# RWKV-7 in a hybrid block: two chunks of the recurrence to a tile, values dumped apart, GpSimd's decay by chunk

## The chip, the cores and the metric

The kernel runs on one core of a Trainium2 chip. Its engines work side by side, each through its own queue in a fixed order: TensorE (PE, with its weight loads as PEld), VectorE (DVE), ScalarE (ACT), GpSimd (POOL) and SyncE (SP), which here does little but start DMAs. The metric is the time of one execution on the device in microseconds, the median of several runs. The profile comes from one further execution.

## The reference

One layer of a block with three mixers (HGRN2, RWKV-7 and MLA attention) and a gated feed-forward part; 512 tokens, width 1024, fp32. The change is in the RWKV-7 mixer, which has 16 heads of size 64:

```python
h = rms_norm(x, mix_pre_g[l])
z = h @ w_cols
o_hg = hgrn2_mixer(...)
o_rw, v_first = rwkv7_mixer(...)
o_mla = mla_mixer(...)
merged = (g_hg * (o_hg @ w_branch[l, 0]) + g_rw * (o_rw @ w_branch[l, 1]) + g_mla * (o_mla @ w_branch[l, 2]))
x = x + rms_norm(merged @ w_out[l], mix_post_g[l])
...
# rwkv7_mixer, for each token t:
sa = einsum('bhvk,bhk->bhv', state, -kk_t)
state = state * w_t + sa[..., None] * (kk_t * a_t) + v_t[..., None] * k_t
y_t = einsum('bhvk,bhk->bhv', state, r_t)
...
y = (group_norm(y) * lnx_g + lnx_b + bonus) * g
```

## The kernel before

Every large product is made of three matmuls, because each fp32 operand is split into a high and a low part (`mm3`, L137 to L141). A weight slab of 256 KB comes by DMA into `wsD`; ScalarE casts the high part `whD` (L207), VectorE subtracts the low part `wlD` (L134). The input projections run as a stream of such groups, with result `mmD`, from the start until about 955 us.

The other work is woven into this stream. The order on each engine is fixed when the kernel is built: instructions carry a priority (a "lane") and a scheduler lays them out; buffers that come free late move what needs them. Two things tie the engines together beyond the data:

- `pace` (L143 to L155) makes GpSimd write a small `token` (L151) after each three dense matmuls, and lets a group start only when the token of the fifth group before it is written (`PACE = 5`). So whatever holds GpSimd holds back the tokens behind it.
- A tile is taken from a pool with a number of buffers. Who writes into a buffer again waits for the last reader of what was in it, a DMA too.

RWKV-7 is computed in chunks of 64 tokens (NC = 8 chunks, C = 64), and the 16 heads go in 8 pairs, two pairs to a group. For each group `rwkv_group` takes a tile `G` (two buffers) that holds for two pairs and all chunks five fields of 128 columns: X (two), LM, PV and BKT. PV has two halves; GpSimd sets the one that will hold the state's part to zero (L449). `rwkv_prep` fills the fields for one pair:

- tile `lw` (one buffer) gets its first column from GpSimd (L527) and the rest from ScalarE (L528);
- GpSimd multiplies BK by the decay of the next chunk (L599), TensorE transposes it, and ScalarE copies it into BKT (L604);
- the gate goes to DRAM (`grw`, L623);
- the values are transposed and copied into PV by ScalarE (L632).

`rwkv_inverse` inverts triangular blocks through DRAM (`Ld`, `Td`, tile `inv`), `rwkv_merge` assembles them in tile `TR`. Then the group's fields are dumped chunk by chunk to `rwd`: 28 DMAs of 640 KB and 4 of 512.

When all groups are done, `rwkv_chain` goes through the 8 chunks in order. `load(c)` fetches one chunk into a tile `CH` (three buffers). In each chunk TensorE makes `z` from X and PV (L714), VectorE copies it to `zsb` (L716), TensorE applies the inverse (L724), and the result goes back into PV: one half by VectorE (L725), the other by ScalarE (L726). From it comes the next chunk's state, which is written into that chunk's PV (L734, L736), and the output `y` (L738, L740). A last loop adds the bonus and multiplies by the gate, both fetched into `CH` tiles.

The attention's rotary angles (L922 to L931) are small VectorE steps that run in this neighbourhood: three steps on `angk`, five or six on `angr`, then a sine on ScalarE; once for sine, once for cosine, on the same two tiles. The program takes RWKV-7's pools (`rwkv_open`) before HGRN2's (`hgrn_open`).

Of the kernel before, what the change touches and what calls it, by code (L numbers as in the profile page):

```python
# [17 lines left out]
ALU = mybir.AluOpType  # L18
# [4 lines left out]
P = 128  # L23
S = 512
# [11 lines left out]
C = 64  # L36
NC = S // C
# [1 line left out]
DECAY = math.exp(-0.5)  # L39
HG_LEVELS = (1, 2, 4, 8, 16)  # L40
HB = 32

RWC = 5 * P
PACE = 5
SCALE = 192.0 ** -0.5

# [58 lines left out]
class Kern:  # L105
# [299 lines left out]
    def rwkv_open(self, e1, e2, e3):  # L405
        tc = self.tc
        pool = lambda es, name, bufs, **kw: es.enter_context(tc.tile_pool(name=name, bufs=bufs, **kw))
        self.gp = pool(e2, "rwG", 1, side="right")
        self.pC, self.pY = (pool(e1, n, 1, space=PSUM, side="right") for n in ("pC", "pY"))
        self.rt = pool(e3, "rt", 1)  # L410
        self.pR = pool(e3, "pR", 2, space=PSUM)


        self.gC = self.t(self.cpool, [P, 8, NC], "gC")
        self.rwd = [self.t(self.dpool, [NC, P, 2, RWC], f"rwd{g}") for g in range(4)]

    def shifted(self, dst, j):

# [22 lines left out]

    def rwkv_group(self, g):

        all_ = self.t(self.gp, [P, 2, NC, RWC], "G", bufs=2)
        G = self.fields(all_)
        G["all"] = all_
        for e in range(2):

            self.nc.gpsimd.memset(G["PV"][e][e * 64:e * 64 + 64], 0.0)  # L449
        G["Ld"] = self.t(self.dpool, [64, 32, 32], "Ld", bufs=2)  # L450
        G["Td"] = self.t(self.dpool, [64, 32, 32], "Td", bufs=2)
        for q in range(2):
            self.lane(5)
            self.rwkv_prep(G, 2 * g + q, q)
        self.lane(3)
        self.rwkv_inverse(G, g)
        self.rwkv_merge(G, g)
        for c in range(NC):
            n = RWC if c < NC - 1 else RWC - P
            self.dumps.append((self.rwd[g][c][:, :, :n], all_[:, :, c, :n]))  # L460
        if g == 3:
            while self.dumps:
                self.nc.sync.dma_start(*self.dumps.pop(0))
# [10 lines left out]

    def fields(self, t):

        return {"X": [t[..., e * P:(e + 1) * P] for e in range(2)], "LM": t[..., 2 * P:3 * P],
                "PV": [t[..., 3 * P + e * C:3 * P + (e + 1) * C] for e in range(2)], "BKT": t[..., 4 * P:]}

    def rwkv(self, e1, e2, e3):  # L480
        self.lane(5)
        self.rwkv_lora()
        self.dumps = []
        for g in range(4):
            self.rwkv_group(g)
        e2.close()
        self.rw = e1.enter_context(self.tc.tile_pool(name="rwC", bufs=1, side="right"))
        self.lane(1)
        self.rwkv_chain()
# [11 lines left out]
    def rwkv_prep(self, G, p, q):  # L501
        nc, rt = self.nc, self.rt
        V, A, Pl = nc.vector, nc.scalar, nc.gpsimd
        ins = self.ins
        H = [slice(0, 64), slice(64, 128)]
        f = slice(p * P, (p + 1) * P)
# [19 lines left out]
        lw = self.t(rt, [P, NC, C + 1], "lw")  # L526
# [11 lines left out]
        gC = self.gC[:, p]  # L538
# [28 lines left out]
        BK = self.t(rt, [P, NC, P], "BK")  # L567
        X = G["X"]
# [13 lines left out]
        LM = G["LM"]  # L582
# [9 lines left out]
        for e in range(2):  # L592
            for b in range(2):
                rows = slice(e * 64 + b * 32, e * 64 + b * 32 + 32)
                o = ((q * 2 + e) * 2 + b) * NC
                nc.sync.dma_start(G["Ld"][o:o + NC].rearrange("c s t -> s c t"), LM[rows, q, :, b * 32:b * 32 + 32])

        n = NC - 1
        Pl.tensor_tensor(BK[:, :n], BK[:, :n], gC[:, 1:].unsqueeze(2).to_broadcast([P, n, P]), op=ALU.mult)  # L599
        for cc in range(0, n, 4):  # L600
            m = min(4, n - cc)
            pt = self.t(self.pR, [P, 4, P], "pr")
# [18 lines left out]
        g = self.t(rt, [P, S], "v")  # L621
# [3 lines left out]
        pv = self.t(self.pR, [P, S], "pr")  # L625
        for i in range(NT):
            nc.tensor.transpose(pv[:, i * P:(i + 1) * P], v[:, i * P:(i + 1) * P], self.ident)
        pv4 = pv.rearrange("t (i h d) -> t i h d", i=NT, h=2)
        for e in range(2):
            dst = G["PV"][e][H[1 - e], q].rearrange("t (i j) d -> t i j d", j=2)  # L630
            for j in range(2):
                A.copy(dst[:, :, j, :], pv4[H[j], :, e, :])  # L632

    def rwkv_inverse(self, G, g):

# [23 lines left out]
    def rwkv_merge(self, G, g):  # L659

        nc, LM = self.nc, G["LM"]
        V, A = nc.vector, nc.scalar
        TR = self.t(self.gp, [P, 2, NC, 32], "TR")
        pR = self.t(self.pY, [P, 2, NC, 32], "yb")
        pM = self.t(self.pY, [P, 2, NC, 32], "yb")
        R = [[slice(e * 64 + o, e * 64 + o + 32) for o in (0, 32)] for e in range(2)]
        qc = [(q, c) for q in range(2) for c in range(NC)]
        for r0, _ in R:
            V.transpose(TR[r0], LM[r0, :, :, 0:32])
        self.side_by_side(  # L670
            partial(nc.tensor.matmul, pR[r1, q, c, :], lhsT=LM[r0, q, c, 32:64], rhs=TR[r0, q, c, :], start=True, stop=True,
                    tile_position=(r0.start, r1.start))
            for q, c in qc for r0, r1 in R)
        for _, r1 in R:
            A.copy(TR[r1], pR[r1])
        self.side_by_side(
            partial(nc.tensor.matmul, pM[r0, q, c, :], lhsT=TR[r1, q, c, :], rhs=LM[r1, q, c, 32:64], start=True, stop=True,
                    tile_position=(r1.start, r0.start))
            for q, c in qc for r0, r1 in R)
        for r0, _ in R:  # L680
            A.copy(LM[r0, :, :, 32:64], pM[r0])

    def rwkv_chain(self):

        nc, rw = self.nc, self.rw
        V, A, Pl = nc.vector, nc.scalar, nc.gpsimd
        mm = nc.tensor.matmul
        H = [slice(0, 64), slice(64, 128)]
        heads = [(p, e) for p in range(8) for e in range(2)]
        chunks = []  # L690

        def load(c):
            t = self.t(rw, [P, 8, RWC], "CH", bufs=3)
            n = RWC if c < NC - 1 else RWC - P
            for g in range(4):
                nc.sync.dma_start(t[:, 2 * g:2 * g + 2, :n], self.rwd[g][c][:, :, :n])
            chunks.append(self.fields(t))

        load(0)
        St = self.t(rw, [P, 8, C], "St")  # L700
# [1 line left out]
        for c in range(NC):  # L702
            if c < NC - 1:
                load(c + 1)
            G = chunks[c]
# [38 lines left out]
                self.lane(1)  # L744
        self.lane(3)

        bv, gr, out = (self.t(rw, [P, 8, RWC], "CH", bufs=3) for _ in range(3))
        for p in range(8):
            nc.sync.dma_start(bv[:, p, :S], self.bv[p])
            nc.sync.dma_start(gr[:, p, :S], self.grw[p])  # L750
        for p in range(8):
            pt = self.t(self.pC if p % 2 else self.pY, [P, S], "zus" if p % 2 else "yb")
            for i in range(NT):
                nc.tensor.transpose(pt[:, i * P:(i + 1) * P], y[:, i, p].rearrange("t e d -> t (e d)"), self.ident)
            o = out[:, p, :S]
            o4 = o.rearrange("f (i j t) -> f i j t", j=2, t=C)
            pt4 = pt.rearrange("f (i j t) -> f i j t", j=2, t=C)
            lb, lg = self.vec("rwkv_lnx_b", p), self.vec("rwkv_lnx_g", p)
            A.activation(o[H[0]], pt[H[0]], AF.Identity, bias=lb[H[0]], scale=lg[H[0]])
            for j in range(2):  # L760

                A.activation(o4[H[1], :, j, :], pt4[H[1], :, 1 - j, :], AF.Identity, bias=lb[H[1]], scale=lg[H[1]])
            V.tensor_tensor(o, o, bv[:, p, :S], op=ALU.add)
            V.tensor_tensor(o, o, gr[:, p, :S], op=ALU.mult)
            nc.sync.dma_start(self.orw[p], o)
            self.dump(f"orw{p}", o)

# [515 lines left out]
    def run(self):  # L1283
        self.full = True
        self.lane(7)
        self.setup()
        es = self.ctx
        self.stream_open(es)
        pes, bes = ExitStack(), ExitStack()
        self.stream_psum(pes, 2)  # L1290
        self.norm_in()
        self.dense_z(RW_OFF + 3072, halves=True)
        for n in range(0, 1024, 256):
            for o in (1024, 0, 2048):
                self.dense_z(RW_OFF + o + n)
            for o in (HG_OFF[1], HG_OFF[0], HG_OFF[2], HG_OFF[3]):
                self.dense_z(o + n)
        for o, n in ((0, 256), (256, 256), (512, 192)):
            self.dense_z(CQ_OFF + o, n)
        for n in (*range(8, 16, 2), *range(0, 8, 2), *range(16, 24, 2)):  # L1300
            self.dense_gate(n)
        e1, e2, e3, e4, e5, oes = (ExitStack() for _ in range(6))
        self.rwkv_open(e1, e2, e3)
        self.hgrn_open(e4)
        self.rwkv(e1, e2, e3)
        for h in range(8):
# [51 lines left out]
```

## Time and profile before

| | |
|---|---|
| median of 3 runs | 1423.61 us (1423.25 to 1424.04) |
| profiled execution, its own time | 1427.17 us |
| its span, first to last instruction | 1425.4 us |
| mean granted clock of TensorE | 0.986 of full speed |
| busy: PE, DVE, ACT, POOL | 96%, 60%, 45%, 12% of the span |
| DMA | 235.80 MB, 165 GB/s |

Times in the trace count from the span's start. A row of the timeline reads: start, duration, engine, line, operation, result <- operands, shape, count; in brackets stands the idle time of the engine before it and what ended it. `q` behind an engine's name is its sequencer, which waits, branches and starts DMAs. The granted clock is given in tenths of full speed on the page and as a fraction of it for a stretch of time.

### The profile page before, as it was taken

How to read it: one execution, taken by the hardware profiler on the slowest of the kernel's cores; microseconds unless marked ns; L12 is line 12 of the kernel's file. 1: busy time of each engine (PE TensorE's matmuls, PEld its weight loads, DVE VectorE, ACT ScalarE, POOL GpSimd, SP SyncE). 2: the span in 40 equal slices, each digit the busy share in tenths (PEclk: the TensorE clock that was granted, in tenths of full speed). 3: DMA queues.
4: the chain of work that ended last, by engine and by line, in shares of the span. 5: the costliest groups of instructions: out<-in, count | busy, mean ns of one | idle time of the engine just before them, and what ended most of it. 6: DMA issues, size and time to landing. Idle time of an engine off the chain costs nothing.

```text
span 1425.4 us, 27298 instructions
## 1 busy us (share of the span) xinstructions
PE 1365.3 (96%) x9664; PEld 1110.6 (78%) x9664; DVE 853.2 (60%) x1756; ACT 638.5 (45%) x1259; POOL 165.6 (12%) x1000
## 2 busy tenths in 40 slices
PE   6999989898999999999999999999999999999998
PEld 6777667676767777778788888887788888888886
DVE  5666888795787784465556376665465344443234
ACT  5553545555455553333565354453354333332222
POOL 3112111121111211223110000001010000000000
PEclk9999999999999999999899999999999999999999
DMA  6564467557556758987466465404544333334232
GB/s 191 150 182 131 123 178 240 171 150 225 176 156 178 249 161 262 403 291 228 152 193 191 147 188 161 152 27 151 196 134 141 98 97 100 98 97 155 96 97 103
DMA packets 186424, 235.80 MB, mean 165 GB/s; under 512 B 34096, under 2 KB 126768, under 8 KB 186288
## 3 DMA queue, kind: packets, MB, share of 16 engines
q1 hardware_dynamic: 184896, 230.92, 51.5%
q10 hardware_dynamic: 1392, 3.15, 0.7%
q8 instruction: 76, 1.25, 0.4%
q14 instruction: 60, 0.49, 0.1%
HBM read 171.75 MB, written 62.26 MB: 164 GB/s over the span
## 4 chain that ended last, share of the span: by engine, by line
PE 74%; DMA 10%; DVE 8%; ACT 4%; issue 3%; SPq 1%; POOL 0%; DVEq 0%; POOLq 0%; ACTq 0%
PE mmD L139 17%; PE mmD L140 16%; PE mmD L141 16%; PE po L139 3%; PE po L141 3%; PE po L140 3%; DVE wlD L134 1%; DMA wsD<-in_w_in_dram 1%; PE pm L139 1%; PE pm L140 1%; PE pm L141 1%; PE pmo L1130 1%; DMA zr<-z 1%; PE pr L196 1%; DMA z<-zst 1%
## 5 line engine op out<-in xcount | busy, mean ns | idle before, releaser
L139 PE MATMUL mmD<-xH,whD 128*128 128x512 f32 (+1 forms) x1232 | 488.0, 398 | 11.5 <-POOL token L151 5.0
L140 PE MATMUL mmD<-xL,whD 128*128 128x512 f32 (+1 forms) x1232 | 477.3, 388 | 0.0
L141 PE MATMUL mmD<-xH,wlD 128*128 128x512 f32 (+1 forms) x1232 | 472.6, 387 | 1.4 <-DVE wlD L134 1.1
L134 DVE TENSOR_TENSOR wlD<-wsD,whD 128x512 fp32r<-128x512 f32 x384 | 264.7, 690 | 293.6 <-ACT whD L207 277.2
L207 ACT CAST whD<-wsD 128x512 fp32r<-128x512 f32 x384 | 236.8, 618 | 363.9 <-PE mmD L140 227.7
L139 PEld LDWEIGHTS mmD<-xH,whD 128*128 128x128 f32 x1232 | 233.5, 190 | 62.5 <-issue 9.0
L141 PEld LDWEIGHTS mmD<-xH,wlD 128*128 128x128 f32 x1232 | 233.6, 190 | 49.6 <-DVE wlD L134 2.8
L140 PEld LDWEIGHTS mmD<-xL,whD 128*128 128x128 f32 x1232 | 234.5, 190 | 40.8
L151 POOL MEMSET token<- 1x1 f32 x912 | 82.0, 90 | 724.0 <-PE mmD L141 708.1
L140 PE MATMUL po<-wlD,fH 128*128 128x512 f32 x176 | 68.7, 390 | 0.0
L141 PE MATMUL po<-whD,fL 128*128 128x512 f32 x176 | 68.6, 390 | 0.0
L139 PE MATMUL po<-whD,fH 128*128 128x512 f32 x176 | 62.0, 390 | 0.0
L281 POOL TENSOR_TENSOR rrs<-rtm,mhalf 128x1 f32<-128x1 f32 x8 | 4.4, 551 | 402.8 <-DVE rtm L276 402.8
L239 ACT COPY zst<-mmD 128x512 f32<-128x512 f32 x64 | 37.4, 584 | 21.9 <-PE mmD L141 21.6
L649 DVE TENSOR_TENSOR invtmp<-inv 64x30 f32<-64x30 f32 (+14 forms) x120 | 38.4, 320 | 14.6 <-DMA inv<-Ld 12.6
L650 DVE TENSOR_TENSOR inv<-inv,invtmp 64x30 f32<-64x30 f32 (+14 forms) x120 | 40.3, 336 | 2.3
L139 PEld LDWEIGHTS po<-whD,fH 128*128 128x128 f32 x176 | 33.1, 188 | 7.1
L141 PEld LDWEIGHTS po<-whD,fL 128*128 128x128 f32 x176 | 33.1, 188 | 7.0
L140 PEld LDWEIGHTS po<-wlD,fH 128*128 128x128 f32 x176 | 33.0, 188 | 7.0
L835 PEld LDWEIGHTS ph<-hq,hk 128*32 128x32 f32 x1536 | 17.5, 113 | 21.4 <-issue 13.0
L835 PE MATMUL ph<-hq,hk 128*32 128x32 f32 x1536 | 23.3, 200 | 5.4 <-DVE hk L860 3.1
L1121 ACT ACTIVATE mp<-pm,mmx,scq 128x128 f32<-128x128 f32 (+3 forms) x32 | 19.8, 620 | 18.9 <-DVE mmx L1118 18.8
(349 smaller groups left out, 1962.7 us busy)
## 6 DMA issues: line engine op xcount, KB each, us to landing
wsD<-in_w_in_dram SPq DMA_DIRECT2D x176, 256.0 KB, 3.3
wsD<-in_w_ffn_in_dram SPq DMA_DIRECT2D x96, 256.0 KB, 2.8
rwd<-G SPq DMA_DIRECT2D x28, 640.0 KB, 6.1
CH<-rwd SPq DMA_DIRECT2D x28, 640.0 KB, 8.5
z<-zst SPq DMA_DIRECT2D x63, 256.0 KB, 3.2
wsD<-in_w_branch_dram SPq DMA_DIRECT2D x48, 256.0 KB, 2.9
wsD<-in_w_ffn_out_dram SPq DMA_DIRECT2D x44, 256.0 KB, 2.6
zr<-z SPq DMA_DIRECT2D x26, 256.0 KB, 3.2
```

The costliest lines, as they stand in the source:

```text
L134: (eng or self.nc.vector).tensor_tensor(dst, src, high.bitcast(F32), op=ALU.subtract)
L139: first = mm(ps, lhsT=lh, rhs=rh, start=start, stop=False)
L140: mm(ps, lhsT=lh, rhs=rl, start=False, stop=False)
L141: return first, mm(ps, lhsT=ll, rhs=rh, start=False, stop=stop)
L151: token = self.nc.gpsimd.memset(self.token, 0.0).ins
L196: last = c()
L207: nc.scalar.copy(h, st)
L239: self.nc.scalar.copy(st[:m], ps)
L649: V.tensor_tensor(tv, cv, rv, op=ALU.mult)
L650: V.tensor_tensor(U[:, :j, j + 1:], U[:, :j, j + 1:], tv, op=ALU.add)
L835: mm(g[b:b + HB, o // P, :], lhsT=k[:, t], rhs=q[:, t], start=True, stop=True)
L1121: A.activation(p[:, :n], s_, AF.Exp, bias=mx, scale=self.scq[:, i:i + 1], accum_out=sm)
```

## The change

- `G` loses the field PV: four fields, 512 columns for each pair and chunk instead of 640. GpSimd's zeroing of it goes.
- The values are copied by ScalarE into a tile that shares the buffer of `lw`, and go by one DMA for each pair (256 KB, in pieces of 256 bytes) to a new DRAM array `rvd`.
- GpSimd's decay is seven instructions, one for each chunk, instead of one.
- The pool of `G` lives until the chain is over. The chain takes its chunks two to a tile from the same two buffers, and PV from two buffers of its own, which two DMAs a chunk fill from `rvd`; GpSimd zeroes the other half for the first chunk alone. The last loop uses the same buffers.
- `TR` moves to the pool of the preparation, which is closed before the chain; HGRN2's pools are taken before RWKV-7's.

```diff
-        self.gp = pool(e2, "rwG", 1, side="right")
+        self.gp = pool(e1, "rwG", 1, side="right")
...
-        self.rwd = [self.t(self.dpool, [NC, P, 2, RWC], f"rwd{g}") for g in range(4)]
+        self.rwd = [self.t(self.dpool, [NC, P, 2, 4 * P], f"rwd{g}") for g in range(4)]
+        self.rvd = self.t(self.dpool, [NC, P, 8, C], "rvd")
...
-        all_ = self.t(self.gp, [P, 2, NC, RWC], "G", bufs=2)
+        all_ = self.t(self.gp, [P, 2, NC, 4 * P], "G", bufs=2)
         G = self.fields(all_)
-        G["all"] = all_
-        for e in range(2):
-
-            self.nc.gpsimd.memset(G["PV"][e][e * 64:e * 64 + 64], 0.0)
...
-            n = RWC if c < NC - 1 else RWC - P
+            n = 4 * P if c < NC - 1 else 3 * P
             self.dumps.append((self.rwd[g][c][:, :, :n], all_[:, :, c, :n]))
...
-        e2.close()
+        e3.close()
         self.rw = e1.enter_context(self.tc.tile_pool(name="rwC", bufs=1, side="right"))
...
-        Pl.tensor_tensor(BK[:, :n], BK[:, :n], gC[:, 1:].unsqueeze(2).to_broadcast([P, n, P]), op=ALU.mult)
+        for c in range(n):
+            Pl.tensor_scalar(BK[:, c], BK[:, c], gC[:, c + 1:c + 2], None, op0=ALU.mult)
...
+        vs = self.t(rt, [P, NC, C], "lw")
         for e in range(2):
-            dst = G["PV"][e][H[1 - e], q].rearrange("t (i j) d -> t i j d", j=2)
+            dst = vs[H[1 - e]].rearrange("t (i j) d -> t i j d", j=2)
             for j in range(2):
                 A.copy(dst[:, :, j, :], pv4[H[j], :, e, :])
+        nc.sync.dma_start(self.rvd[:, :, p].rearrange("c t d -> t c d"), vs)
...
-        TR = self.t(self.gp, [P, 2, NC, 32], "TR")
+        TR = self.t(self.rt, [P, 2, NC, 32], "TR")
...
         def load(c):
-            t = self.t(rw, [P, 8, RWC], "CH", bufs=3)
-            n = RWC if c < NC - 1 else RWC - P
+
+            if c % 2 == 0:
+                self.two = self.t(self.gp, [P, 2, 8, 4 * P], "G", bufs=2)
+            t = self.two[:, c % 2]
+            n = 4 * P if c < NC - 1 else 3 * P
             for g in range(4):
                 nc.sync.dma_start(t[:, 2 * g:2 * g + 2, :n], self.rwd[g][c][:, :, :n])
-            chunks.append(self.fields(t))
+            t = self.fields(t)
+            pv = self.t(rw, [P, 2, 8, C], "PV", bufs=2)
+            t["PV"] = [pv[:, e] for e in range(2)]
+            for e in range(2):
+                nc.sync.dma_start(pv[H[1 - e], e], self.rvd[c, H[1 - e]])
+                if c == 0:
+                    Pl.memset(pv[H[e], e], 0.0)
+            chunks.append(t)
...
-        bv, gr, out = (self.t(rw, [P, 8, RWC], "CH", bufs=3) for _ in range(3))
+        two, out = (self.t(self.gp, [P, 2, 8, S], "G", bufs=2) for _ in range(2))
+        bv, gr, out = two[:, 0], two[:, 1], out[:, 0]
...
+        self.hgrn_open(e4)
         self.rwkv_open(e1, e2, e3)
-        self.hgrn_open(e4)
```

The instructions of TensorE, VectorE and ScalarE are as many as before. Their places change on all engines up to the end of the chain; from there on the order is the same. Three places follow. A row names line, operation, result and operands (each with the number of its buffer), shape and count; the lines of the changed kernel differ from those before by a few.

GpSimd in the third group's first half, before: the decay (L599), a step of HGRN2, the diagonal of the inverse (L643), the zeroing of the next `G` (L449), and the first column of `lw` (L527) at the start of the next half.

```order
L599 TENSOR_TENSOR BK_5365<-BK_5365,gC_4650 128x896
L151 MEMSET token 1x1 x5
L281 TENSOR_TENSOR hrs_7921<-htm_7920,mhalf 128x4
L151 MEMSET token 1x1 x2
L643 MEMSET inv_5466 64x32
L151 MEMSET token 1x1 x7
L449 MEMSET G_5612 64x16x64 x2
L151 MEMSET token 1x1 x19
L281 TENSOR_TENSOR rs_5664<-ss_5662,mhalf 128x8
L151 MEMSET token 1x1 x17
L527 MEMSET lw_5795 128x8
```

The same stretch of GpSimd now:

```order
L594 TENSOR_SCALAR BK_5386<-BK_5386,gC_4658 128x128 x4
L149 MEMSET token 1x1 x5
L594 TENSOR_SCALAR BK_5386<-BK_5386,gC_4658 128x128
L279 TENSOR_TENSOR hrs_8000<-htm_7999,mhalf 128x4
L594 TENSOR_SCALAR BK_5386<-BK_5386,gC_4658 128x128 x2
L149 MEMSET token 1x1 x6
L640 MEMSET inv_5495 64x32
L149 MEMSET token 1x1 x12
L521 MEMSET lw_5663 128x8
L149 MEMSET token 1x1 x8
L279 TENSOR_TENSOR rs_5691<-ss_5689,mhalf 128x8
L149 MEMSET token 1x1 x24
```

The two memsets of `G` are gone, the decay comes in pieces, and the memset of `lw` stands ahead of `rs` with twelve tokens behind the inverse.

VectorE at the chain's last chunk, before: the cosine's half of the angles (`angk`, `angr`) stands between the sums into the last PV (L736) and the copies `zsb` (L716) and into PV (L725).

```order
L922 TENSOR_SCALAR angk_10227<-anga_10226 128x128
L923 TENSOR_SCALAR angk_10227<-angk_10227 128x128
L924 TENSOR_SCALAR angk_10227<-angk_10227 128x128
L925 SCALAR_TENSOR_TENSOR angr_10228<-angk_10227,anga_10226 128x128
L926 SCALAR_TENSOR_TENSOR angr_10228<-angk_10227,angr_10228 128x128
L927 SCALAR_TENSOR_TENSOR angr_10228<-angk_10227,angr_10228 128x128
L929 TENSOR_SCALAR angr_10228<-angr_10228 128x128
L930 TENSOR_SCALAR angr_10228<-angr_10228 128x128
L716 COPY zsb_7313<-zus_7296 128x512
L725 COPY CH_7197<-zus_7332 64x8x64
```

VectorE at the last chunk now: `hst`, `htm` and `hsg` are HGRN2's, the first row is the sum into the last PV.

```order
L743 TENSOR_TENSOR PV_7279<-zus_7339,St_6630 64x512 x2
L274 TENSOR_SCALAR htm_9355<-hss_9354 128x4
L132 TENSOR_TENSOR wlD_4130<-wsD_4127,whD_4129 128x512
L723 COPY zsb_7393<-zus_7376 128x512
L905 SCALAR_TENSOR_TENSOR hsg_9170<-ph_9368,hon,hsg_9170 128x512
L132 TENSOR_TENSOR wlD_4160<-wsD_4157,whD_4159 128x512
L732 COPY PV_7279<-zus_7412 64x512
L933 SCALAR_TENSOR_TENSOR angr_10305<-angk_10304,anga_10303 128x128
```

The steps on `angr` for the cosine stand behind the last copy into PV; those for the sine stand before the chain's first `zsb`. On ScalarE, the sine's table load, the sine (L939) and three more casts stand directly ahead of the last copy into the other half of PV (L733).

SP in the second group's first half (the third pair), now: the loads of the inverse back into `G` (L654), the gate's DMA, the new DMA of the values, and what follows.

```order
L654 DMA G_4683<-Td_4685 32x8x32 x7
L239 DMA z_1615<-zst_1613 128x512
L654 DMA G_4683<-Td_4685 32x8x32
L618 DMA grw<-v_5314 128x512
L629 DMA rvd_4663<-lw_5322 128x8x64
```

Before, the first four stood there in the same order, with a small weight for the next pair behind them. The next half group's `lw` is written after this DMA has read the buffer.

More of the change, by code (lines that the diff above doesn't have):

```diff
@@ L41 @@
 HB = 32
-RWC = 5 * P
 PACE = 5
@@ L475, in fields @@
     def fields(self, t):
-        return {"X": [t[..., e * P:(e + 1) * P] for e in range(2)], "LM": t[..., 2 * P:3 * P],
-                "PV": [t[..., 3 * P + e * C:3 * P + (e + 1) * C] for e in range(2)], "BKT": t[..., 4 * P:]}
+        return {"X": [t[..., e * P:(e + 1) * P] for e in range(2)], "LM": t[..., 2 * P:3 * P], "BKT": t[..., 3 * P:]}
     def rwkv(self, e1, e2, e3):
@@ L745, in rwkv_chain @@
         self.lane(3)
-        bv, gr, out = (self.t(rw, [P, 8, RWC], "CH", bufs=3) for _ in range(3))
+        two, out = (self.t(self.gp, [P, 2, 8, S], "G", bufs=2) for _ in range(2))
+        bv, gr, out = two[:, 0], two[:, 1], out[:, 0]
         for p in range(8):
-            nc.sync.dma_start(bv[:, p, :S], self.bv[p])
-            nc.sync.dma_start(gr[:, p, :S], self.grw[p])
+            nc.sync.dma_start(bv[:, p], self.bv[p])
+            nc.sync.dma_start(gr[:, p], self.grw[p])
         for p in range(8):
@@ L754, in rwkv_chain @@
                 nc.tensor.transpose(pt[:, i * P:(i + 1) * P], y[:, i, p].rearrange("t e d -> t (e d)"), self.ident)
-            o = out[:, p, :S]
+            o = out[:, p]
             o4 = o.rearrange("f (i j t) -> f i j t", j=2, t=C)
@@ L762, in rwkv_chain @@
                 A.activation(o4[H[1], :, j, :], pt4[H[1], :, 1 - j, :], AF.Identity, bias=lb[H[1]], scale=lg[H[1]])
-            V.tensor_tensor(o, o, bv[:, p, :S], op=ALU.add)
-            V.tensor_tensor(o, o, gr[:, p, :S], op=ALU.mult)
+            V.tensor_tensor(o, o, bv[:, p], op=ALU.add)
+            V.tensor_tensor(o, o, gr[:, p], op=ALU.mult)
             nc.sync.dma_start(self.orw[p], o)
```

## Prediction

> **What bounds the kernel now.** The page comes first: the span, busy time by engine, the granted clock in slices, and the chain that ended last.
>
> ```profile
> span 1425.4 us, 27298 instructions
> PE 1365.3 (96%) x9664; PEld 1110.6 (78%) x9664; DVE 853.2 (60%) x1756; ACT 638.5 (45%) x1259; POOL 165.6 (12%) x1000
> PEclk9999999999999999999899999999999999999999
> PE 74%; DMA 10%; DVE 8%; ACT 4%; issue 3%; SPq 1%; POOL 0%; DVEq 0%; POOLq 0%; ACTq 0%
> ```
>
> TensorE is busy for 1365.3 of 1425.4 us, so 60.1 us is idle. The number of its instructions is the same before and after. So the change can act on the time in two ways only: by the places where TensorE idles, and by the stretches in which it runs at half clock. The next views are therefore TensorE's waits by length, and the line that paces it.
>
> ```profile
> PE mmD L139 <- POOL token L151: 5.0, 3, 2.7
> PE zus L724 <- DVE zsb L716: 4.6, 2, 2.4
> ```
> ```profile
> 214.81 0.09 POOL L151 MEMSET token<- 1x1 f32 x1 [0.60 <-PE mmD L141]
> 215.49 0.09 POOL L151 MEMSET token<- 1x1 f32 x1 [0.59 <-PE mmD L141]
> ```
>
> The first two rows give total, count and longest. The tokens come 0.68 to 0.69 us apart, one for three dense matmuls, and a group needs the token five groups back. So GpSimd may be held up for about 5 x 0.69 = 3.45 us before dense work stops. That is the slack I use below. The two longest waits are looked at in time.
>
> **Stall one: GpSimd's memset.** The rows are GpSimd's, then TensorE's, then the stretches before and after (length, then busy time of PE, PEld, DVE, ACT, POOL; granted clock; DMA share; GB/s).
>
> ```profile
> 266.83 1.94 POOL L449 MEMSET G<- 64x1024 f32 x2 [6.25 <-DMA rwd<-G]
> ...
> 389.41 1.94 POOL L449 MEMSET G<- 64x1024 f32 x2 [3.04 <-DMA rwd<-G]
> ```
> ```profile
> 265.83 0.39 PE L141 MATMUL mmD<-xH,wlD 128*128 128x512 f32 x1
> 268.97 0.50 PE L139 MATMUL mmD<-xH,whD 128*128 128x512 f32 x1 [2.75 <-POOL token L151]
> ```
> ```profile
> 255.00:270.02 15.02, 11.41 (x83) 8.32 (x82) 10.09 (x30) 5.32 (x11) 3.03 (x15) 1.00 0.65 206
> 270.02:276.85 6.83, 6.83 (x49) 4.61 (x48) 6.45 (x15) 3.69 (x8) 0.35 (x4) 0.50 0.87 263
> ```
>
> A group's tile may be zeroed only when the dump out of it has landed. GpSimd stood 6.25 us behind that and needed 1.94 more, together 8.2, far over the slack; TensorE idled 2.75 us. One microsecond after it resumed, the clock fell to 0.50 for 6.83 us. Work at half speed costs half of the stretch: 3.4 us. At 389.41 the same memset held GpSimd for 5.0 us, and no wait of TensorE came of it: there it had enough unpaced work to do.
>
> **Stall two: a copy behind the angles on VectorE.**
>
> ```profile
> 687.46 0.29 DVE L925 SCALAR_TENSOR_TENSOR angr<-angk,anga 128x128 f32<-128x128 f32 x1 [1.65 <-ACT sin L931]
> ...
> 688.95 0.69 DVE L716 COPY zsb<-zus 128x512 f32<-128x512 f32 x1
> ```
> ```profile
> 685.82 1.28 ACT L931 ACT_TABLE_LOAD   x1
> 687.12 0.31 ACT L931 ACTIVATE sin<-angr 128x128 f32<-128x128 f32 x1
> ```
> ```profile
> 689.70 0.59 PE L724 MATMUL zus<-zsb,CH 64*64 64x64 f32 x8 [2.43 <-DVE zsb L716]
> ```
> ```profile
> 681.00:689.86 8.86, 6.31 (x96) 5.52 (x98) 6.31 (x18) 5.98 (x11) 0.09 (x1) 1.00 0.91 299
> 689.86:700.10 10.24, 10.24 (x87) 8.87 (x86) 2.00 (x7) 3.18 (x5) 1.84 (x4) 0.50 0.26 79
> ```
>
> The chain's last chunk needs `zsb`. VectorE's queue has the cosine half of the angle work ahead of it; that half overwrites the sine's argument, so it waits for ScalarE's sine, which waits for its table. TensorE idles 2.43 us, and then 10.24 us run at 0.50: 5.1 us more.
>
> **The change, part by part.** The profiled execution took 1427.17 us; all steps are against it.
>
> 1. *The memsets of G go.* The new tile is first written by VectorE's masks in the group's second half, long after the dump. Nothing of GpSimd stands there, so nothing is late next. Stall one goes whole: −2.75 − 3.4 = **−6.2 us**. The other six memsets waited in no row that reached TensorE: 0.
> 2. *The angles move.* In the new order on VectorE the first half of the angle work stands before the chain's first `zsb`; the second half stands behind the chain's last copy into PV. The last `zsb` has only HGRN2 steps, slab subtractions and the PV sums ahead of it. Stall two goes: −2.43 − 5.1 = **−7.5 us**. Late next is ScalarE's half of the last PV copy: its queue now has the sine's table load and the sine ahead, 1.28 + 0.31 us, and then three casts. TensorE has tiny and dense matmuls to do there. Between 0 and 2.4 us (the wait it replaces); I take **+1.0**, from the 1.6 us of table and sine less part cover.
> 3. *The values go through DRAM.* Eight more DMAs of 256 KB, in 256-byte pieces, read the `lw` tile. The next half group's memset of `lw` (GpSimd) and its write (ScalarE) now wait until that landed, seven times. Behind the memset stand the pace tokens, behind the write ScalarE's slab casts. The trace lacks this transfer; the nearest rows, and the time there was between the last value copy and the next write of `lw`:
>
> ```profile
> DMA packets 186424, 235.80 MB, mean 165 GB/s; under 512 B 34096, under 2 KB 126768, under 8 KB 186288
> grw<-v SPq DMA_DIRECT2D x8, 256.0 KB, 3.4
> inv<-Ld SPq DMA_DIRECT2D x4, 256.0 KB, 4.9
> ```
> ```profile
> 252.39 6.05 DMA inv<-Ld
> ```
> ```profile
> 209.03 1.50 ACT L632 COPY G<-pr 64x256 f32<-64x256 f32 x4
> ...
> 214.29 0.63 ACT L528 ACTIVATE lw<-t 128x512 f32<-128x512 f32 x1
> ```
> ```profile
> 211.03 3.29 SPq L657 DMA_DIRECT2D G<-Td  x7
> ...
> 215.33 0.48 SPq L623 DMA_DIRECT2D grw<-v  x1
> ```
>
>    The copies end at 210.53 and the write starts at 214.29, 3.8 us later. Landing takes 3.4 us for the same size, 6.05 at worst; issued at once, it would hold the write by −0.4 to 2.3 us. But SP sends in order: here the loads of the inverse stood ahead, and the DMA before the new one went out at 215.33. The new one would follow at 215.81 and land at 219.2, so ScalarE's hold is 4.9 us. This is the first half of a group, while the inverse of the group before comes back: three of the seven places; at the others SP is freer. GpSimd is covered for 3.45 us, ScalarE by the slabs cast ahead. Three times 1.45 us are 4.4 if nothing else covers; 0 is the other bound. I take **+2.0 us**, near the middle; a hold at all seven is the last rival.
> 4. *GpSimd's decay in seven pieces.*
>
> ```profile
> L599 POOL TENSOR_TENSOR BK<-BK,gC 128x896 f32<-128x896 f32 x8 | 15.6, 1955 | 9.2 <-PE pr L196 5.5 <-DVE hF L862 2.9 <-DVE inv L650 0.7
> L281 POOL TENSOR_TENSOR rrs<-rtm,mhalf 128x1 f32<-128x1 f32 x8 | 4.4, 551 | 402.8 <-DVE rtm L276 402.8
> L449 POOL MEMSET G<- 64x1024 f32 x8 | 7.5, 948 | 9.7 <-DMA rwd<-G 9.3 <-POOLq L1343 0.3
> ```
>
>    One 128x128 piece with a scalar does not occur. By size it is 1955/7 = 279 ns; the smallest tensor operation here takes 551, a token 90. Seven are 0.6 to 3.9 us against 1.96, in blocks of four and three with tokens between. The longest block is 4 x 0.55 = 2.2 us, within the slack, and at 279 it is 1.1. The transposes can start after four pieces rather than after all. I take 0, by the size.
> 5. *The chain's loads.* Chunks come in two-chunk tiles, with PV in 16 further DMAs. The first load of PV stands on SP's queue some five paced groups (3.45 us) ahead of the first matmul that reads it; by the 3.4 us above it lands just then. Bounds 0 and 2.6 (6.05 less 3.45); I take **+0.5**. The chain's own two chunk buffers ahead remain.
> 6. *Fewer bytes and moved pools.* The 32 dumps and the 32 loads shrink by 128 KB each, 4 MB each way, and the values add 2 MB each way; in sum 2 MB less each way of the 235.80 MB moved. It lies beside a TensorE that is 96% busy: 0.
>
> Sum: −6.2 − 7.5 + 1.0 + 2.0 + 0.5 = −10.2 us. 1427.17 − 10.2 = 1417.0. The profiled execution was 3.56 us above the median of the runs shown, 1423.61; with the same distance the forecast is **1413.4 us**.
>
> **The rivals.** B: *the clock does not follow these gaps.* For it speaks a stretch at half clock with no idle ahead; against it, that it followed the two longest waits within 1.1 us.
>
> ```profile
> 215.00:218.82 3.82, 3.80 (x110) 3.18 (x109) 3.38 (x6) 2.66 (x5) 0.18 (x2) 1.00 0.76 227
> 218.82:222.20 3.38, 3.38 (x9) 2.60 (x10) 3.34 (x8) 3.31 (x6) 0.18 (x2) 0.50 0.59 181
> ```
>
> If the low stretches stay or come again elsewhere, only the idle time comes back: −2.75 − 2.43 + 3.5 = −1.7, so 1421.9. [...]
>
> C: *the order is laid anew and as much waits elsewhere.* All of TensorE's order up to the chain shifts by some groups, and most of the 60 us of idle time is in short waits, which can fall otherwise and lengthen by what the two long ones gave. Then nothing changes: 1423.6.
>
> D, the other side: *the landing of the values holds GpSimd and ScalarE.* One mechanism, seven places. If the hold is x, TensorE idles x − 3.45 us each time, and a clock stretch of 3.4 us adds 1.7. With the −13.7 of both stalls gained and nothing else, it reaches the old time at x = 5.4 without the clock (13.7/7 = 1.96 above the slack), at 3.7 with it. At x = 4.9, the hold worked out above: 7 x (1.45 + 1.7) = 22.1, so 1423.6 − 13.7 + 1.5 + 22.1 = 1433.5; at 6.05 it would be 1441.5. Against it: the hold at 389.41 of 5.0 us cost TensorE nothing, and the write of `lw` already came 3.8 us after the copies. [...]
>
> **How the numbers follow.** Chances: forecast 0.48, B 0.19, C 0.13, D 0.20. The low end is where three other low stretches go too and the +3.5 does not come:
>
> ```profile
> 351.90:358.70 6.80, 5.71 (x16) 4.67 (x17) 3.73 (x6) 1.23 (x2) 1.04 (x9) 0.50 1.00 337
> 611.40:614.80 3.40, 3.40 (x49) 3.03 (x48) 2.89 (x6) 0.94 (x2) 1.50 (x1) 0.51 1.02 381
> ```
>
> (6.80 + 3.40 + 3.38)/2 = 6.8, and 1413.4 − 6.8 − 3.5 = 1403. The high end, 1431, takes in B, C and D's lower third; some 0.13 lie above and 0.06 below. A measurement of this kernel tells some 0.2%, 2.85 us, from no change: faster means under 1420.8, slower over 1426.4. Faster, 0.56: 0.46 of the forecast, 0.08 of B, 0.02 of C. Slower, 0.23: 0.18 of D, 0.05 of C and B. The rest, 0.21, is no change.
>
> **What would show it.** Right: no GpSimd idle behind a dump near 267, no wait of `zus` for `zsb` over 2 us at the chain's end, and the mean clock above 0.986 by the 8.5/1425 = 0.006 of half-clock work saved. Wrong: idle time of GpSimd ahead of the `lw` memset, or of ScalarE ahead of the `lw` write, put down to the DMA into the value array, with TensorE waiting for tokens right after (D); the same number of low stretches at other places (B); a new wait of over 2 us with another name (C).

## The result and the profile after

| | before | changed |
|---|---|---|
| median | 1423.43 us (1421.02 to 1424.04, 4 runs) | 1408.7 us (1403.39 to 1412.37, 4 runs) |
| profiled execution / span | 1427.17 / 1425.4 us | 1408.42 / 1406.6 us |
| mean granted clock | 0.986 | 0.996 |

The ratio is 0.9893, with a 95% interval of 0.9865 to 0.9920: 1.1% faster, 14.7 us by the medians, where 10.2 were forecast. The page of the changed kernel (busy time, clock in slices), then the row groups of GpSimd's decay and two of TensorE's waits (total, times, longest):

```profile
span 1406.6 us, 27356 instructions
PE 1354.8 (96%) x9664; PEld 1103.2 (78%) x9664; DVE 848.3 (60%) x1756; ACT 638.6 (45%) x1259; POOL 190.8 (14%) x1042
...
PEclk9999999999999999999999999999999999999999
```
```profile
L594 POOL TENSOR_SCALAR BK<-BK,gC 128x128 f32<-128x128 f32 x56 | 47.0, 854 | 11.8 <-PE pr L194 11.8
```
```profile
PE mmD L137 <- POOL token L149: 5.6, 6, 1.8
...
PE zus L721 <- DMA PV<-rvd: 2.1, 1, 2.1
```

TensorE's busy time fell by 10.5 us with the same 9664 matmuls. Its low stretches, at 0.50, ahead of the one at the very end add up to 34.1 us before and 10.2 now; at half of their length, an estimate, some 12 us of half clock are gone. Its idle time fell by 8.3 us, from 60.1 to 51.8. The decay costs 854 ns a piece where I had 279. No wait of 2.7 us for a token is left, but the waits for tokens add up to 5.6 us where they were 5.0: they are more and shorter. And the chain's first chunk waits 2.1 us for its values.

One more figure is used below. Each run comes with its mean granted clock. In the trace of before, dense matmuls start 0.43 us apart in the low stretch behind 270.02 and 0.23 us apart after it, so this low stretch, full of work, lost nearly half its length. (1 − clock) x span is then an estimate of what the half clock cost in that run; for the profile of before this is 0.014 x 1425.4 = 20.0 us. It is called **clock loss** here, and the time less this loss **the rest**. Medians over the runs of each kernel, for before over all 72 runs beside the experiments:

| kernel | median us | ratio to before (95%) | clock loss | rest |
|---|---|---|---|---|
| before | 1422.6 | | 17.0 | 1405.7 |
| changed | 1408.7 | 0.9893 (0.9865 to 0.9920) | 7.0 | 1401.5 |
| e1 zeroing late | 1422.9 | 1.0003 (0.9987 to 1.0019) | 17.1 | 1406.6 |
| e2 angles behind | 1419.4 | 0.9976 (0.9956 to 0.9995) | 14.2 | 1403.3 |
| e3 both | 1416.4 | 0.9959 (0.9943 to 0.9976) | 12.8 | 1405.0 |
| e4 pool order | 1418.2 | 0.9958 (0.9944 to 0.9971) | 12.8 | 1405.6 |
| e5 decay whole | 1413.4 | 0.9938 (0.9917 to 0.9960) | 11.3 | 1402.7 |
| e6 values in own tile | 1408.1 | 0.9891 (0.9870 to 0.9912) | 9.1 | 1398.2 |
| e7 decay in pieces | 1419.1 | 0.9980 (0.9963 to 0.9998) | 17.7 | 1401.7 |
| e8 filled wait | 1424.0 | 1.0016 (1.0002 to 1.0031) | 15.6 | 1408.1 |
| e9 without the route | 1413.9 | 0.9936 (0.9915 to 0.9958) | 14.1 | 1400.2 |
| e10 zeroing back | 1408.3 | 0.9899 (0.9872 to 0.9926) | 7.0 | 1401.0 |
| e11 changed again | 1405.6 | 0.9883 (0.9856 to 0.9910) | 7.0 | 1399.1 |
| e12 own tile, angles | 1404.3 | 0.9884 (0.9856 to 0.9912) | 9.8 | 1395.7 |

By this split 10 us of the gain are clock loss, and 4.2 (by e11 6.6) are the rest. The split is rough, and rather too high on the clock's side: over 187 runs, all those of the table, with each kernel's mean taken off, the time moves by only 0.57 us for each us of clock loss. (A run of before with a clock of 0.94 is left out of this; its 1422.02 us were no longer than the others'.) At 0.57, 10 us of clock loss would be 5.7 us of time. And the two sets of the changed kernel, which are the same program, differ by 2.4 us in the rest, where e11 was expected within 1.5. So some 6 to 10 us of the gain are half clock, and a difference of the rest of under some 2.5 us shows nothing. Gains of single edits below are the ratio's part of 1422.6 us.

### The profile page after: what moved, and what is told of

Its sections match the earlier page's. It is cut to its first block, busy times and chain, and to the rows that moved or that the text cites. A ratio compares the mean times of both kernels' runs of the same rounds, so it can differ in the third digit from the quotient of the medians.

```text
span 1406.6 us, 27356 instructions
## 1 busy us (share of the span) xinstructions
PE 1354.8 (96%) x9664; PEld 1103.2 (78%) x9664; DVE 848.3 (60%) x1756; ACT 638.6 (45%) x1259; POOL 190.8 (14%) x1042
## 4 chain that ended last, share of the span: by engine, by line
PE 82%; DMA 6%; DVE 4%; issue 4%; ACT 3%; POOL 1%; SPq 1%; POOLq 0%; DVEq 0%; ACTq 0%
PE mmD L137 18%; PE mmD L138 17%; PE mmD L139 17%; PE po L137 4%; PE po L139 4%; PE po L138 4%; PE pr L194 1%; DMA wsD<-in_w_in_dram 1%; DMA z<-zst 1%; DMA zr<-z 1%; PE pmo L1138 1%; PE pm L137 1%; PE pm L139 1%; PE pm L138 1%; PE ph L843 1%
## 5 line engine op out<-in xcount | busy, mean ns | idle before, releaser
L646 DVE TENSOR_TENSOR invtmp<-inv 64x30 f32<-64x30 f32 (+14 forms) x120 | 38.7, 322 | 17.7 <-DMA inv<-Ld 16.0
L594 POOL TENSOR_SCALAR BK<-BK,gC 128x128 f32<-128x128 f32 x56 | 47.0, 854 | 11.8 <-PE pr L194 11.8
L1136 ACT COPY mpT<-pmt 128x128 f32<-128x128 f32 (+3 forms) x32 | 13.6, 425 | 38.0 <-PE pmt L1134 37.9
```

The lines of the kernel that those rows point to most:

```text
L594: Pl.tensor_scalar(BK[:, c], BK[:, c], gC[:, c + 1:c + 2], None, op0=ALU.mult)
L646: V.tensor_tensor(tv, cv, rv, op=ALU.mult)
```

## The experiments

### The two long waits, one by one (e1, e2, e3) and the pool order alone (e4)

e1, in the kernel before:

```diff
-        for e in range(2):
-            self.nc.gpsimd.memset(G["PV"][e][e * 64:e * 64 + 64], 0.0)
...
-            self.rwkv_prep(G, 2 * g + q, q)
+            last = self.rwkv_prep(G, 2 * g + q, q)      # its last copy into PV
+            for e in range(2 if q == 0 else 0):
+                m = self.nc.gpsimd.memset(G["PV"][e][e * 64:e * 64 + 64], 0.0)
+                self.tc.add_manual_dep(m.ins, last.ins.name, ...)
```

> The kernel before, with GpSimd's zeroing of each group's tile moved behind the first half of the preparation; nothing else. Theory 1 (the two long stalls, each with the half-clock stretch behind it, carry the gain): the wait at 267 us and the half clock at 270 go, 2.75 + 3.4 = 6.2 us, so about 1417.3 against 1423.4. Theory 2 (the clock does not follow the gap): 2.75 us, so 1420.7, and a low stretch near 270 or soon after stays. Theory 3 (the gain comes from the new order as a whole): within 1 us of before.

e2, in the kernel before:

```diff
-            V.tensor_copy(PV[0][H[0]], z[H[0]])
+            self.last_pv = V.tensor_copy(PV[0][H[0]], z[H[0]])
...
-            V.tensor_scalar(k, ang, 1.0 / (2 * math.pi), turn, op0=ALU.mult, op1=ALU.add)
+            first = V.tensor_scalar(k, ang, 1.0 / (2 * math.pi), turn, op0=ALU.mult, op1=ALU.add)
+            if turn:
+                self.tc.add_manual_dep(first.ins, self.last_pv.ins.name, ...)
```

> The kernel before, with the cosine's half of the angle work tied behind the chain's last copy into PV; nothing else. Theory 1: the wait of 2.43 us for zsb at 687 us and the 10.24 us at half clock go, 7.5 us, so about 1415.9 against 1423.4. Theory 2 (idle time alone): 2.4 us, so 1421.0, with a low stretch near 690 still there. Theory 3: within 1 us of before.

e3 has both edits.

> The kernel before with both edits: zeroing behind the first half, cosine's half behind the last copy into PV. Theory 1: the two add up, 13.7 us, so about 1409.7, as fast as the changed kernel (1408.7) although none of its tiles, DMAs or decays is in it. Theory 2: 5.2 us, 1418.2. Theory 3: no more than 2 us off 1423.4.

e4, in the kernel before:

```diff
+        self.hgrn_open(e4)
         self.rwkv_open(e1, e2, e3)
-        self.hgrn_open(e4)
...
-        e4.close()
         e3.close()
+        e4.close()
```

> The kernel before with HGRN2's pools taken before RWKV-7's and released after them; nothing else. The sine's half of the angles then stands before the chain's first zsb, the cosine's half still before the last. Theory 1: the cosine's half no longer waits for the table, so zsb's wait at the chain's end and its clock stretch go (up to 7.5 us), the memset's stall near 267 stays: about 1416 to 1418. Theory 3 (the order as a whole): the full gain, near 1409.

e1 gained nothing (1.0003, 0.9987 to 1.0019): theory 1 falls for the memset, and so does theory 2; only theory 3's time came. Its longest wait for a token is 1.4 us, yet the half clock is not gone. In e1 a low stretch follows another wait of TensorE, some 10 us further on; the waits' row, that of the timeline, and stretches of 3.41 us:

```profile
PE mmD L139 <- POOL token L151: 3.1, 3, 1.4
```
```profile
279.14 1.36 PE L554 MATMUL pr<-cst,t 128*128 128x2 f32 x8 [1.72 <-ACT t L550]
```
```profile
276.31:279.72 3.41, 1.69 (x11) 1.15 (x10) 2.53 (x8) 3.40 (x6) 0.18 (x2) 1.00 0.15 52
279.72:283.14 3.42, 3.42 (x42) 2.63 (x42) 2.83 (x8) 1.01 (x2) 0.00 (x0) 0.50 0.28 72
```

The same windows in the kernel before, on both stalls of the forecast:

```profile
266.61:270.02 3.41, 1.05 (x5) 0.88 (x6) 2.47 (x7) 0.61 (x1) 2.34 (x7) 1.00 0.92 281
270.02:273.43 3.41, 3.41 (x41) 1.95 (x40) 3.02 (x8) 2.93 (x7) 0.18 (x2) 0.50 0.80 256
686.45:689.86 3.41, 0.98 (x12) 0.89 (x13) 2.02 (x6) 2.30 (x5) 0.00 (x0) 1.00 1.00 368
689.86:693.27 3.41, 3.41 (x41) 3.29 (x39) 0.68 (x1) 0.92 (x2) 0.00 (x0) 0.50 0.11 39
```

The first number after the length is TensorE's busy time. In each pair the first window has TensorE working for half of its time or less, 1.05, 0.98 and 1.69 of 3.41 us, and the next is granted 0.50. In the traces of before and of the changed kernel all low stretches of one trace begin at multiples of 3.41 us from each other, and all but the one at the very end last for such multiples (3.41, 6.83 and 10.24 us). So in these traces the clock goes with TensorE's work in a window of fixed place, and whether a wait was followed by 0.50 went with where it fell in that raster and with what else was in the window; how often is counted below.

e4 shows this with the memset's stall itself, which stayed in it. The wait is as long as before, but a line of the raster, 264.18, falls into it; TensorE is busy for 2 us on either side, and the clock stays:

```profile
265.57 0.50 PE L139 MATMUL mmD<-xH,whD 128*128 128x512 f32 x1 [2.71 <-POOL token L151]
```
```profile
260.77:264.18 3.41, 2.10 (x19) 1.23 (x7) 3.21 (x10) 1.21 (x3) 0.74 (x1) 1.00 0.81 280
264.18:267.60 3.42, 2.03 (x10) 1.45 (x11) 2.97 (x7) 1.75 (x3) 1.78 (x9) 1.00 0.74 239
267.60:271.01 3.41, 3.41 (x48) 2.58 (x45) 3.28 (x9) 2.47 (x6) 0.27 (x3) 1.00 0.90 275
```

The 14 profiles kept, cut into such windows from 8 us on, have 5633 at full clock. Where TensorE was busy for less than 0.4 of the window, the next one ran at half clock in 18 of 18 cases; from 0.4 to 0.5 in 20 of 24, from 0.5 to 0.6 in 9 of 46, and above that in 17 of 5545. The longest waits that fall in the three windows of little work above were 2.75 and 2.43 us (before) and 1.72 us (e1).

e2 gained 3.4 us (0.7 to 6.3): theory 1's 7.5 is out, theory 2's 2.4 is not. The wait for `zsb` at the chain's end went, but not the half clock. Timeline and windows of e2 there:

```profile
684.76 2.72 PE L996 MATMUL pm<-ones,msq 128*128 128x1 f32 x12
687.41 1.97 PE L724 MATMUL zus<-zsb,CH 64*64 64x64 f32 x32
```
```profile
676.61:680.02 3.41, 3.34 (x27) 2.71 (x22) 1.89 (x5) 2.88 (x5) 0.18 (x1) 1.00 0.32 91
680.02:683.43 3.41, 2.28 (x43) 2.31 (x45) 2.96 (x8) 3.36 (x6) 0.00 (x0) 0.50 0.94 288
683.43:686.85 3.42, 3.42 (x37) 3.30 (x34) 0.43 (x1) 1.26 (x4) 0.00 (x0) 0.50 1.00 344
686.85:690.26 3.41, 3.41 (x40) 3.28 (x40) 0.79 (x2) 0.61 (x2) 0.00 (x0) 0.50 0.37 141
690.26:693.67 3.41, 3.41 (x13) 3.10 (x13) 2.80 (x13) 2.70 (x4) 0.77 (x2) 0.50 0.11 38
```

`zus` starts with no wait behind `pm`. Still 17 us run at half clock, and the window ahead of them was busy for 3.34 of 3.41 us. It held sixteen `pm` with one column each (1.95 us) and five dense matmuls; behind it come 1.2 us of idle, small matmuls and more `pm`. Here 3.34 us of busy time, 1.95 of them with one column to a matmul, did not keep the clock. That is no rule: in 15 of the 17 busy windows counted last 34 or more matmuls start, where dense work has some 15; but 958 windows that were busy for over 0.6 with as many kept the clock.

e3 gained 5.8 us (3.3 to 8.1) where the two terms made 13.7. That is near theory 2's 5.2, but not in its way: the clock loss fell by 4 us and the rest hardly. e4 gained 6.0 (4.1 to 8.0), near the 1416 to 1418 that theory 1 had for it. As expected, its last `zus` no longer waits for `zsb`, and the memset's stall stayed. But the clock stretch at the chain's end, which theory 1 took away, is there: 6.8 us from 677.19 on. By the table e4's gain is clock loss (17.0 to 12.8), with the rest unchanged.

### The filled wait (e8)

```diff
             z = self.t(self.pC, [P, 8, C], "zus")
+            for i in range(3 if c == NC - 1 else 0):
+                mm(z.rearrange("p a b -> p (a b)"), lhsT=self.ident, rhs=LM[:, 4 * (i % 2):4 * (i % 2) + 4, :], ...)
```

> The kernel before with three matmuls of 128x512 added ahead of the last chunk's product with the inverse; their result is overwritten. They fill TensorE's wait of 2.43 us at 687 us and remove no wait. Theory W (the clock is set by how much TensorE works in a window of 3.4 us, so a filled wait costs no clock): the 10.24 us at half clock near 690 go or shrink to one window, 3.4 to 5.1 us faster, about 1418 to 1420. Rival (the clock falls for another reason than the idle time, or the tiny matmuls around it are enough): the stretch stays, and the time is the same or up to 2 us longer.

This one is not a test of what it was meant for. TensorE's row shows why:

```profile
689.56 2.84 PE L724 MATMUL zus<-CH,cst 128*128 128x512 f32 x6 [2.39 <-DVE zsb L716]
```

`zus` has one buffer, which `zsb` is copied from; so the added matmuls waited with the rest and added 2.84 us behind the wait. The rest is 2.4 us longer, and the time by its ratio 2.3 (0.3 to 4.4), where theory W had 3.4 to 5.1 less. In this profile no low stretch follows at 690, with the same wait. The windows of the raster:

```profile
687.66:691.07 3.41, 1.51 (x4) 0.79 (x5) 1.71 (x5) 0.96 (x3) 0.00 (x0) 1.00 0.72 271
691.07:694.49 3.42, 3.42 (x46) 2.35 (x44) 0.68 (x1) 0.24 (x1) 0.00 (x0) 1.00 0.00 0
```

Busy for 1.51 us with the added full-size matmuls, the window kept the clock, where 1.69 us with smaller ones in e1 lost it. This is one window in one execution, and the size of the matmuls is not shown to decide: in e3 a window with six of 128x512 lost it.

```profile
267.64:271.05 3.41, 1.43 (x6) 1.24 (x7) 2.36 (x6) 2.79 (x6) 0.09 (x1) 1.00 0.69 233
271.05:274.46 3.41, 3.41 (x9) 2.65 (x8) 3.41 (x10) 1.94 (x4) 0.26 (x3) 0.50 0.86 241
```

Over all runs of e8 the clock loss fell by 1.4 us, within the scatter.

### GpSimd's decay (e5, e7)

e5 puts the single instruction back into the changed kernel; e7 puts the seven into the kernel before.

```diff
-        for c in range(n):
-            Pl.tensor_scalar(BK[:, c], BK[:, c], gC[:, c + 1:c + 2], None, op0=ALU.mult)
+        Pl.tensor_tensor(BK[:, :n], BK[:, :n], gC[:, 1:].unsqueeze(2).to_broadcast([P, n, P]), op=ALU.mult)
```

> The changed kernel with GpSimd's decay as one instruction again, all else as changed. In the changed kernel's profile the 56 pieces take 47.0 us against 15.6 for the eight whole ones, a block of four 2.4 us or more. Theory A (the pieces hold the pace tokens): the undo is 1 to 3 us faster than 1408.7. Theory B (the pieces let the transposes start early and fill TensorE's windows): the undo is 2 to 5 us slower, by half clock that comes back near 200 us. Theory C (the order as a whole decides, no part by itself): the time moves by the half-clock stretches, either way, with the idle and working time within 2 us.

> The kernel before with GpSimd's decay in seven pieces, all else as before. Theory A: 1 to 3 us slower than 1423, from tokens held up. Theory B: 2 to 5 us faster, the half clock near 200 to 220 us goes. Theory C: by less than 2 us either way without the half clock.

e5 is slower, 1413.4 against 1408.7 and 1405.6; alone (e7) the pieces give 0.2% (0.02 to 0.37), 2.8 us. Theory A falls: although they keep GpSimd busy three times as long (43.7 us in e7 against 15.6), they help. Theory B's amounts are about met: 2 to 5 us were expected of each, and 4.7 (by e11 7.8) and 2.8 came. So is its place, in the profiles: of the seven with the whole decay six have a low stretch between 195 and 220 us, of the seven with the pieces none. But in e7 the clock loss over all runs is no smaller than before (17.7 against 17.0), and its gain is in the rest, 4 us. One place that can give it: VectorE and GpSimd at one place, before and then in e7:

```profile
195.75 2.17 DVE L823 SCALAR_TENSOR_TENSOR hsg<-hsg,hz 128x512 f32<-128x512 f32 x1
...
198.05 0.67 DVE L840 TENSOR_TENSOR hq<-hq,hf 128x512 f32<-128x512 f32 x1
```
```profile
198.77 0.46 PE L835 MATMUL ph<-hq,hk 128*32 128x32 f32 x32 [1.13 <-DVE hq L840]
```
```profile
193.09 0.67 DVE L824 SCALAR_TENSOR_TENSOR hsg<-hsg,hz 128x512 f32<-128x512 f32 x1
```
```profile
190.98 4.21 POOL L600 TENSOR_SCALAR BK<-BK,gC 128x128 f32<-128x128 f32 x3 [0.73 <-PE pr L196]
```

Beside the whole decay VectorE's step on `hsg` took 2.17 us, and `hq`, which TensorE waits for, came late. Beside the pieces it takes 0.67, and it is GpSimd that is held (three pieces in 4.21 us, where the median of one is 0.60 in the changed kernel). The mean of its eight (before, then e7):

```profile
L823 DVE SCALAR_TENSOR_TENSOR hsg<-hsg,hz 128x512 f32<-128x512 f32 x8 | 7.1, 883 | 8.1 <-ACT hsg L822 8.1
```
```profile
L824 DVE SCALAR_TENSOR_TENSOR hsg<-hsg,hz 128x512 f32<-128x512 f32 x8 | 5.5, 689 | 7.3 <-ACT hsg L823 7.3
```

In six of the seven profiles with the whole decay this mean is 875 to 911 ns (e4: 690), in all seven with the pieces 684 to 690. That the two engines hold each other is read from these durations; why they do wasn't tested. The step on `hsg` is not all that the pieces give: e9 below adds them to e4, where it was not held, and its rest is 5.4 us shorter than e4's. What the earlier start of the transposes adds (theory B) wasn't tested apart.

### The values' tile (e6, e12)

```diff
-        vs = self.t(rt, [P, NC, C], "lw")
+        vs = self.t(rt, [P, NC, C], "vs")
```

> The changed kernel with the values staged in a tile of their own, so that neither GpSimd nor ScalarE waits for their landing; all else as changed. In the changed kernel GpSimd stood 18.4 us in 5 waits behind it. Theory A (the waits cost TensorE, as the term of +2.0 us had it): 1 to 4 us faster than 1408.7. Theory B (covered by the slack): within 1 us in idle and working time; what is left moves with the half-clock stretches.

In the changed kernel GpSimd waited for the landing five times, up to 5.7 us (the waits' row, then the longest in time):

```profile
POOL lw L521 <- DMA rvd<-lw: 18.4, 5, 5.7
```
```profile
451.07 0.12 POOL L521 MEMSET lw<- 128x8 f32 x1 [5.71 <-DMA rvd<-lw]
```

In e6 no such wait is left. But the time is no shorter, 1408.1 against 1408.7 and 1405.6 in the two sets of the changed kernel, so theory A is not shown. The rest is 1 to 3 us shorter, which would fit the term of 2.0 us but is about what the two sets differ by; the clock loss is 2 us larger. The order had shifted too: the cosine's half stands ahead of the last `zsb` again, though in e6's profile no `zus` waits for it there and no low stretch follows. e12 ties it behind, with e2's edit:

> The changed kernel with the values in a tile of their own and the cosine's half of the angles tied behind the chain's last copy into PV (staging the values apart had moved it ahead of the last zsb). If both terms of the forecast hold, it has neither the wait for the landing nor the one for zsb: 1 to 4 us faster than the changed kernel, about 1405 to 1407. If they are covered: the same as the changed kernel within 2 us.

1404.3 us, with the lowest rest of all, 1395.7, but 2.8 us more clock loss than the changed kernel. Against before it is 0.9884; the changed kernel beside it on the chip has 0.9883. So no gain is shown over the changed kernel.

### What is left of the change without its new tiles (e9), the zeroing put back (e10), and the changed kernel again (e11)

e9 is the kernel before with the edits of e1, e4 and e7.

> The kernel before with three small parts: HGRN2's pools first, the decay in seven pieces, GpSimd's zeroing behind the first half. The values stay in the group's tile, the chain's chunks one to a tile. Theory P (these parts carry the change; by the runs so far 4.7 us for the pools, 2.5 to 3.5 for the pieces, 0 for the zeroing): about 1414 to 1416 against 1422.5. Theory R (the rest of the gain, some 6 us, needs the new tiles and the route of the values): no faster than 1414. Theory S (only single waits count): the full 14.7 us, 1408.

e10, in the changed kernel:

```diff
+        for e in range(2):
+            self.nc.gpsimd.memset(G["X"][e][e * 64:e * 64 + 64, :, :, 0:64], 0.0)
```

> The changed kernel with GpSimd zeroing 64x1024 twice at each group's start again, as before, in a part of the tile that is written over later; so it waits again for the dump out of the tile. Step 1 of the forecast: 6.2 us slower, a wait of TensorE for a token of over 2 us near 260 to 270 us and half clock after it. Rival (by the first run, where taking the zeroing away gave nothing: another wait takes its place in the same window): within 2 us of the changed kernel.

> The changed kernel unaltered, beside the others on one chip, for its time apart from its half clock: 1408.7 by four runs, of which 7.0 us are half clock. By the theory that idle and working time are set by the order and the rest by the clock, the part without the loss is 1401.5 within 1.5 us, and the runs differ by the loss.

e9 reaches the rest of the changed kernel (1400.2), but not its clock: 9.1 of 15.2 us by the ratios, with 14.1 us of clock loss. Its 1413.9 us lie where the ranges of theories P and R meet, so the number does not choose between them; theory S falls. The three parts add up: 6.0 us for the pools (e4), 2.8 for the pieces (e7) and 0 for the zeroing (e1) are 8.8 of the 9.1. What is missing, 6.1 us of time with 7 us of clock loss, comes with the new tiles, the route of the values or the place of the cosine's half, which were not told apart.

e10 is within noise of the changed kernel, 1408.3 against 1408.7 and 1405.6, and step 1's 6.2 us do not come back. The memsets stand in GpSimd's queue again, ahead of the same steps. But in this order GpSimd stood at most 4.7 us ahead of them, where it had been 6.25, and TensorE's longest wait for a token stays at 1.8 us. The stall did not come back with the memsets, so e10 shows that they cost nothing by themselves, and not what the stall cost:

```profile
POOL G L446 <- ACT whD L205: 4.7, 1, 4.7
...
POOL G L446 <- DMA bv<-t: 3.1, 1, 3.1
```
```profile
PE mmD L137 <- POOL token L149: 6.1, 7, 1.8
```

## The prediction, step by step

The direction and the amount were as forecast, and roughly the form: −8.5 us of clock and −1.7 of the rest were written, −10.0 and −4.2 came by the split above. That the amount fits is luck in good part. The two stalls, 13.7 us in the sum, gave 5.8 together in e3; the pieces of the decay, which the sum has at 0, and some 6 us that no run explains made up for it.

**Step 1, the memset's stall (−6.2): wrong.** It read one wait and the low stretch behind it as one price that goes with the wait. e1 took the wait away from the kernel before for 0. The low stretch did follow the window with the wait in it, but the price did not hang on the wait alone: in e4 the same wait cost no clock, and in e1 a window further on was short of work instead. In the changed kernel TensorE's waits for tokens are 5.6 us in all after 5.0.

**Step 2, the angles (−7.5): in part.** e2, which ties the cosine's half behind, gives 3.4 us; e4, the order of pools by which the change itself moves the sine's half, gives 6.0. The wait of 2.43 us went in both, as forecast; the low stretch at the chain's end did not hang on it, since e2's profile has 17 us of it and e4's 6.8 without that wait. In the changed kernel there are dense matmuls between the tiny ones there, and that place runs at full clock:

```profile
674.30:677.70 3.40, 3.38 (x46) 2.79 (x43) 1.44 (x2) 2.17 (x5) 0.07 (x1) 1.00 0.61 189
677.70:681.10 3.40, 3.27 (x26) 3.00 (x24) 2.52 (x3) 3.36 (x6) 0.26 (x3) 1.00 0.00 0
681.10:684.50 3.40, 3.40 (x15) 2.82 (x16) 2.39 (x8) 1.77 (x3) 0.32 (x3) 1.00 0.63 200
```

The term of 1.0 us for the last PV copy does not show: no wait for it is among TensorE's.

**Step 3, the values (+2.0): the hold came, its price is not shown.** GpSimd waited for the landing at five of seven places, up to 5.7 us; ScalarE, for whose write the 4.9 us were worked out, waited for it once, 0.7 us. The DMAs took 2.8 to 9.0 us to land, 3.6 in the median, where the forecast's worst was 6.05. Without the hold (e6) the time is no shorter. Rival D needed the hold to stop TensorE at all seven places, and the tokens' waits rose by 0.6 us.

**Step 4, the decay (0): wrong on both counts.** The piece was mis-sized, 854 ns against 279. And it was priced only as a load on GpSimd, whose slack, 3.45 us by its estimate, covers it; the earlier start of the transposes was named and put at nothing. It gains instead: 2.8 us alone, 5 to 8 us in the changed kernel. By the traces a VectorE that is held less may have a part in it; how large, is not shown.

**Step 5, the chain's loads (+0.5): too small.** The rows of SP and TensorE:

```profile
546.93 3.14 SPq L701 DMA_DIRECT2D PV<-rvd  x4
```
```profile
552.62 0.37 PE L721 MATMUL zus<-PV,G 128*64 128x64 f32 x3 [2.11 <-DMA PV<-rvd]
```

The first was sent 3.6 us before TensorE was ready, and what it needed landed 2.1 too late, within the bound of 2.6. In the other direction both waits for `zsb` are gone, 4.6 us in two, of which the forecast had one.

**Rivals.** B is half right. Low stretches did follow windows that are short of work (38 of the 42 under half), but they did not hang on single gaps, as its premise had it; its result, that they stay, did not come: the clock loss fell from 17 to 7 us. The same holds for C, the order as a whole: it is re-laid, but here to the better. In the profiles, the end of the trace aside, five windows of the kernel before have TensorE busy for less than half of the time, two of the changed kernel and none in e11. What stays open is which part of the new order keeps the windows full.

## What to carry over

Where a kernel's clock drops in short stretches, split each run's time into the loss by the clock and the rest before explaining a change, and test how well the split holds on runs of one and the same kernel; the two parts can move apart (in e7 the rest fell by 4.0 us, the loss did not), and a profile shows one draw of the first. A low stretch was not the fixed price of the wait ahead of it (a wait of 2.7 us was followed by one in the kernel before and by none in e4): ask what TensorE does in the whole window, tiny matmuls included, and test by taking only that wait away. GpSimd was busy for 12% of the span, and yet a step of VectorE took 2.17 us beside its whole decay and 0.67 beside the pieces: look at the neighbour's durations also beside an engine that has time to spare.

## What was not expected of the hardware

Before and after the change low stretches start on a raster of 3.41 us, and all but the last of a trace end on it. In the 14 profiles a window with TensorE at work for less than half of it was followed by one at 0.50 in 38 of 42 cases. Of the windows busy for over 0.6 it was 17 of 5545; in e2 one busy for 3.34 of 3.41 us, with 128x1 matmuls for 1.95 of them, was followed by 17 us at 0.50. The same wait of 2.7 us was followed by 0.50 with 2.36 us of it in one window (before), and by full clock where a line of the raster fell into it (e4). The time of the changed kernel ran from 1403.39 us at a clock of 0.998 to 1412.37 at 0.993. A 128x128 multiplication by one scalar for each partition took GpSimd 0.60 us in the median there and up to 2.93 (shortest, median, longest of the 56):

```profile
L594 POOL TENSOR_SCALAR BK<-BK,gC x56: 593/604/2934, 75.8 to 483.5; 128x128 f32<-128x128 f32 x56
```
